# Expert results of a mixture-of-experts layer: rows scattered to token order, instead of tiles stored and gathered

## The chip, the core and the metric

One core of a Trainium2 chip runs one decoder layer for 512 tokens of 1024 values, in float32. The metric is the time of one execution on the device in microseconds (us), the median of several runs. The profile shows one execution on that core. Its engines are TensorE (PE in the rows, its weight loads PEld), VectorE (DVE), ScalarE (ACT), GpSimd (POOL) and SyncE (SP, its queue SPq), and 16 DMA engines that all queues share.

## What is computed

Only the last part of the layer matters here: a mixture of 32 experts in 4 groups of 8. Each token takes the best group and in it the two best experts, so there are 512 x 2 = 1024 (token, expert) rows.

```python
p_group, g_idx = lax.top_k(group_probs, 1)
...
top_vals, top_idx = lax.top_k(sel_logits, TOP_K_IN_GROUP)
weights = jax.nn.softmax(top_vals, axis=-1) * p_group
...
    h = jax.nn.silu(jnp.einsum('nd,edf->nef', t, w_g[sl])) * jnp.einsum('nd,edf->nef', t, w_u[sl])
    h = h * combine[:, sl, None]
    out = out + jnp.einsum('nef,efd->nd', h, w_d[sl])
...
x = layer_norm(DEEPNORM_ALPHA * x + gate2 * moe, ln2_g[l], ln2_b[l])
```

An expert's weights are 3 MB (gate and up 1024 x 256 each, down 256 x 1024).

## The kernel before

Attention and the first norm run until about 510 us, then the routing, then the experts. The routing sorts the 1024 rows by expert. Experts 0 to 5 have fixed places; the others are put in order of their number of rows, on the chip.

The experts are worked off in 12 units (line 124): eight pairs, whose tile of 128 rows is 64 of each of two experts, and four quads, with 32 of each of four. A unit has `ntl` tiles: three for most, two for the pair `pairs[7]` and for the quads 2 and 3. Tile 0 is always computed. Tiles 1 and 2 are computed under a condition (`tiles`, line 1278): only if the largest number of rows of an expert in the unit, read from `fl`, exceeds what the tiles before hold. ScalarE and VectorE work on all tiles in any case (`act_h`, `h_copy`, `y_evac`, lines 1228 to 1264); those of a tile not computed hold nothing that is read later. Rows beyond an expert's third tile go through a loop for overflow (line 1469), which runs only if there are any.

For each unit (loop at line 1381): `gate_up` (line 1224), `act_h`, transposes `h_tr` and their copies `h_copy` (1247), `down` (1254), and `y_evac` (1264), which multiplies by `gate2` and puts tile t into the buffer `yb[t]`. There is one such buffer for each t, shared by all units. Where a pair follows a pair, `gate_up` of the next unit is put ahead of the unit's transposes.

The weights go through 15 granules of 1 MB (`load_gran`, lines 862 and 865); each is loaded again when its matmuls are done. All these loads are issued by SP, with conditions for experts without rows.

TensorE, SP and GpSimd run this stage in the order in which the code is written (`manual_schedule(engines=MS)`, lines 1194 and 1332). The order of VectorE and ScalarE is chosen by a scheduler at compile time, except in the last unit. An engine whose next instruction waits runs nothing behind it. Semaphores are put in by the framework, from the accesses to each tile.

Results travel so:

- `Ys`, a tensor in DRAM, has a row for each place of each tile, and 640 rows for the overflow loop. `zero_fill` (133) writes zeros into all rows that may stay unwritten; SP issues it between the attention heads.
- `y_store0` (1270) and `y_store` (1276) store `yb[0]`, and `yb[1]` and `yb[2]` under a condition, on SP's queue, in between the weight loads. The last unit is not stored: it is added from `yb` through a selection matrix.
- `y_rows` (1097 to 1123), called in unit 1, computes for each token the two rows of `Ys` that it needs, `posy` and as integers `posyi`.
- At the end GpSimd gathers these rows into `gt`, 128 rows of 4 KB in each of eight indirect DMAs (1518), VectorE adds them with their weights (1538) for one half of the columns, TensorE for the other, and the second norm follows (`moments`, `normed`, `gain`, `shift`).

GpSimd has besides in this stage: `norm_rows` (line 1294, small loads) and `select_rows` (1308 to 1315, the selection matrix of the last unit), both called at the end of the loop's pass for unit 9, and `scaled` (1460) at the end. VectorE's copies `split_rows` (1300) need the loads of `norm_rows`; TensorE's transposes `select_tr` (1321) in the last unit need the selection matrix.

Of the kernel before, what the change touches and what calls it, by code (L numbers as in the profile page):

```python
# [11 lines left out]
F32 = mybir.dt.float32  # L12
F32R = mybir.dt.float32r
BF16 = mybir.dt.bfloat16
# [21 lines left out]
YO = 14 * 192 + 2 * 128 + 8 * 96 + 8 * 64  # L36
NY = YO + 640
QR = 384
# [14 lines left out]
def tile_layer(ctx: ExitStack, tc: tile.TileContext, x, c, positions, w_ada, b_ada, w_in, mla_q_norm_g, w_q_up,  # L53
# [18 lines left out]
    def tmp(tag, shape, dtype=F32, name=None):  # L72
        return mp.tile([P] + shape, dtype, name=name or tag, tag=tag, bufs=2)
# [51 lines left out]

    Ys = dr.tile([NY, D], F32, name="Ys")
    zero = [(u.row + P, (u.ntl - 1) * P) for u in (pairs + quads)[:-1]]
    zero += [(quads[-1].row, P * quads[-1].ntl)] + [(lo, P) for lo in range(YO, NY, P)]

    def zero_fill(n):  # L130
        for lo, m in zero[:n]:
            to = Ys[lo:lo + m, :].rearrange("r (h n) -> (r h) n", h=2).rearrange("(p a) n -> p a n", a=max(1, m // 64))
            SP.dma_start(to, zt[0:min(P, 2 * m)].unsqueeze(1).to_broadcast([min(P, 2 * m), max(1, m // 64), 512]))
        del zero[:n]
# [553 lines left out]

    zero_fill(6)
    branch(w_branch_sb, osh, osl, lambda a, m: DVE.tensor_tensor(part(gat, m), a, part(gat, m), ALU.mult), "ysb")  # L690
# [16 lines left out]

    oml = gran("Q1", [HP, S], F32R, "oml")
    attention(score_mla, vm, omh, oml, 54 / 32.0, 1, before=lambda h: (fq.until(f"qu{h}"), zero_fill(4)))
    fq.drain()  # L710

# [346 lines left out]
    posy = cp.tile([P, NT, 2], F32, name="posy")  # L1058
    posyi = cp.tile([P, NT, 2], I32, name="posyi")

# [34 lines left out]
    def y_rows():  # L1095
# [27 lines left out]
        DVE.tensor_copy(posyi, posy)  # L1123

# [45 lines left out]
    def overflow_list():  # L1170
        over = ovt
        for k in range(TOV):
            lim = float(OV0 + CAP * k)
            DVE.tensor_scalar(over[:, 0, :, k], cnt[:, 0, :], lim, None, ALU.is_gt)
            DVE.tensor_scalar(over[:, 2, :, k], cnt[:, 1, :], lim, None, ALU.add)
            DVE.memset(over[:, 2, 1, k:k + 1], float(NSLOT - CAP) - lim)
            DVE.tensor_scalar(over[:, 3, :, k], cnt[:, 0, :], lim, None, ALU.subtract)
            DVE.tensor_scalar(over[:, 4, :, k], yo[:, 1, :], lim, None, ALU.add)
# [86 lines left out]

    def y_rows_of(u, t):
        return Ys[u.row + P * t:u.row + P * t + P, :]
# [64 lines left out]
    with tc.manual_schedule(engines=MS):  # L1332
# [48 lines left out]
        for n, u in enumerate(units):  # L1381
# [88 lines left out]
    with tc.If(total > 0):  # L1470
        with tc.For_i(0, total) as it:
# [36 lines left out]
            POOL.indirect_dma_start(out=Ys[:, :], out_offset=bass.IndirectOffsetOnAxis(ap=oii[0:64], axis=0), in_=yo[0:64], in_offset=None,  # L1508
                                    bounds_check=NY - 1, oob_is_err=False)


    ALL = MS | {mybir.EngineType.DVE, mybir.EngineType.Activation}
    with tc.manual_schedule(engines=ALL):
        gts = []
        for t in range(NT):
            gt = gran(etags[10 + t], [2, D], F32, f"gt{t}")
            for j in range(2):
                POOL.indirect_dma_start(out=gt[:, j, :], out_offset=None, in_=Ys[:, :],
                                        in_offset=bass.IndirectOffsetOnAxis(ap=posyi[:, t, j:j + 1], axis=0),
                                        bounds_check=NY - 1, oob_is_err=False)  # L1520
            gts.append(gt)
# [134 lines left out]
```

## Time and profile before

| what | value |
|---|---|
| median of 3 runs | 825.21 us (820.85 to 825.68) |
| the profiled execution's own time | 827.33 us |
| its span on the core | 825.6 us |
| mean granted clock of TensorE | 0.929 of full speed |
| TensorE, VectorE, ScalarE, GpSimd busy | 84%, 64%, 30%, 26% of the span |
| DMA packets | 195.15 MB, mean 236 GB/s |

The shares are means over stages that differ. Times in the profile count from the span's start. A busy time of TensorE holds pipelined matmuls, so it is not its use at its peak. In rows of one instruction or of several merged ones the columns are start (us), duration (us), engine, line, operation, output and input, number, and in brackets the idle time just before it with what ended that.

### The profile page before, as it was taken

Reading aid. Unit: us, or ns where it says so; the run is one execution under the profiler, and the core shown is the slowest. Engines: PE = TensorE matmul, PEld = TensorE weight load, DVE = VectorE, ACT = ScalarE, POOL = GpSimd, SP = SyncE. Lnnn points to the kernel's source line nnn. Section 1 sums busy time; section 2 is a strip of 40 time slices with the busy share of each in tenths; the row PEclk is TensorE's granted clock in tenths of the full one; section 3 lists DMA queues with packets and bytes.
Section 4 is the critical chain, followed back from the end, with each engine's and each line's share of the span. In section 5 each row is a group of like instructions: output and inputs, shape, how many; then the busy total and the mean of one; then the engine's idle time right before and its main releaser. Section 6 shows DMA issues by size and latency. Waiting matters only on the chain. (4 is left out here: it accounts for less than half of the span.)

```text
span 825.6 us, 10607 instructions
## 1 busy us (share of the span) xinstructions
PE 691.5 (84%) x3201; PEld 426.7 (52%) x3201; DVE 524.3 (64%) x1083; ACT 249.7 (30%) x545; POOL 217.8 (26%) x269
## 2 busy tenths in 40 slices
PE   5789999999999798999989665777889779977880
PEld 3568877677776464666668553432333223322330
DVE  3995366867746857876596766664834715543297
ACT  2123244333435434443231324342201101111411
POOL 5546022322333312200363440300000000028174
PEclk9999999999999898999999867698999889999995
DMA  9964365547612793331549348788999998899942
GB/s 266 257 178 129 111 223 197 191 153 249 207 32 66 272 363 120 89 124 54 202 180 359 124 144 286 247 292 293 389 410 417 400 415 325 298 357 402 349 183 102
DMA packets 92109, 195.15 MB, mean 236 GB/s; under 512 B 11421, under 2 KB 53498, under 8 KB 86154
## 3 DMA queue, kind: packets, MB, share of 16 engines
q1 hardware_dynamic: 88544, 182.71, 62.5%
q0 software_dynamic: 3424, 11.57, 4.0%
q8 instruction: 36, 0.59, 0.3%
q14 instruction: 31, 0.25, 0.1%
q10 hardware_dynamic: 74, 0.03, 0.0%
HBM read 173.30 MB, written 35.67 MB: 253 GB/s over the span
## 5 line engine op out<-in xcount | busy, mean ns | idle before, releaser
L1224 PE MATMUL pgu<-ex,xT 128*64 128x512 f32 (+1 forms) x608 | 119.5, 615 | 17.7 <-DMA ex<-in_w_exp_up_dram 10.6
L1224 PEld LDWEIGHTS pgu<-ex,xT 128*64 128x64 f32 (+1 forms) x608 | 49.1, 129 | 82.3 <-issue 71.1
L330 PE MATMUL acc<-uh,whi 128*128 128x512 f32 x224 | 90.9, 406 | 0.0
L330 PE MATMUL acc<-uh,wlo 128*128 128x512 f32 x224 | 88.3, 394 | 0.4 <-DVE wlo L321 0.4
L330 PE MATMUL acc<-ul,whi 128*128 128x512 f32 x224 | 87.6, 391 | 0.0
L1254 PE MATMUL py<-ex,hT 128*64 128x512 f32 (+1 forms) x304 | 66.2, 668 | 17.7 <-DVE hT L1247 12.8
L577 POOL TENSOR_TENSOR w<-be,sc 128x128 f32<-128x128 f32 (+3 forms) x32 | 39.6, 1239 | 135.6 <-DVE sc L575 113.0
L1232 ACT ACTIVATE sl<-pgu 128x256 f32<-128x256 f32 x33 | 11.4, 383 | 173.7 <-PE pgu L1224 154.3
L1294 POOL DMA_DIRECT2D lraw<-in_ln_g_dram x4 | 2.0, 510 | 203.2 <-DVE lraw L1291 203.2
L330 PEld LDWEIGHTS acc<-uh,whi 128*128 128x128 f32 x224 | 42.1, 188 | 14.6 <-issue 4.4
L321 DVE TENSOR_TENSOR wlo<-raw,whi 128x1024 fp32r<-128x1024 f32 x27 | 34.4, 1272 | 21.8 <-ACT whi L320 21.6
L330 PEld LDWEIGHTS acc<-uh,wlo 128*128 128x128 f32 x224 | 42.0, 188 | 11.2 <-DVE wlo L321 2.0
L1254 PEld LDWEIGHTS py<-ex,hT 128*64 128x64 f32 (+1 forms) x304 | 16.9, 135 | 59.2 <-issue 29.2
L443 DVE SCALAR_TENSOR_TENSOR macc<-ra,rtx,macc 128x1024 f32<-128x1024 f32 x28 | 38.4, 1394 | 13.5 <-DMA ra<-in_w_ada_dram 13.4
L330 PEld LDWEIGHTS acc<-ul,whi 128*128 128x128 f32 x224 | 42.2, 188 | 7.9 <-issue 0.2
L1233 DVE TENSOR_TENSOR sl<-pgu,sl 128x256 f32<-128x256 f32 x33 | 12.9, 419 | 43.3 <-ACT sl L1232 43.3
L320 ACT CAST whi<-raw 128x1024 fp32r<-128x1024 f32 x27 | 28.4, 1051 | 29.5 <-PE acc L330 14.2
L1247 DVE COPY hT<-phT 128x256 f32<-128x256 f32 x33 | 13.2, 419 | 32.6 <-PE phT L1239 19.7
L575 DVE TENSOR_TENSOR_SCAN sc<-al 128x127 f32<-128x127 f32 (+3 forms) x32 | 27.1, 849 | 10.5 <-ACT al L571 8.6
L817 PE MATMUL oh<-wo,mixh 128*128 128x512 f32 x64 | 28.7, 497 | 5.8 <-DVE wo L801 5.8
L536 PE MATMUL px<-ident,w 128*128 128x128 f32 x160 | 28.9, 280 | 5.3 <-POOL w L577 2.1
L1217 DVE COPY xT<-XRA 128x128 f32 (+1 forms) x30 | 7.6, 252 | 34.7 <-PE pgu L1224 29.7
(491 smaller groups left out, 1515.5 us busy)
## 6 DMA issues: line engine op xcount, KB each, us to landing
ex<-in_w_exp_gate_dram SPq DMA_DIRECT2D x64, 512.0 KB
ex<-in_w_exp_up_dram SPq DMA_DIRECT2D x64, 512.0 KB
ex<-in_w_exp_down_dram SPq DMA_DIRECT2D x32, 1024.0 KB
ra<-in_w_ada_dram SPq DMA_DIRECT2D x16, 1024.0 KB
raw<-in_w_in_dram SPq DMA_DIRECT2D x12, 1024.0 KB
Ys<-dq SPq DMA_DIRECT2D x10, 1024.0 KB
ada<-in_w_ada_dram SPq DMA_DIRECT2D x16, 512.0 KB
rwo<-in_w_out_dram SPq DMA_DIRECT2D x6, 1024.0 KB
```

The costliest lines, as they stand in the source:

```text
L320: ACT.copy(hi, w)
L321: DVE.tensor_tensor(lo, w, hi.bitcast(F32), ALU.subtract)
L330: PE.matmul(a, w_[:, k, :], part(u_, k), start=(k == 0 and n == 0), stop=(k == nk - 1 and n == 2))
L443: DVE.scalar_tensor_tensor(o, v, cact[:, k, 0:1], o, ALU.mult, ALU.add)
L536: PE.transpose(px[:, kt * P:(kt + 1) * P], w[:, kt * P:(kt + 1) * P], ident)
L575: DVE.tensor_tensor_scan(sc[:, 0:W - 1][:, ::-1], al[:, 1:W][:, ::-1], al[:, 1:W][:, ::-1], 1.0, ALU.mult, ALU.bypass)
L577: POOL.tensor_tensor(w[:, 0:W], be[:, 0:W], sc[:, 0:W], ALU.mult)
L817: PE.matmul(a, u_, w_[:, k % 4, :], start=first and n == 0, stop=last and n == 2)
L1224: PE.matmul(ps_t[rows, :], xT[u, t][:, k, rows], ew[e, k // 4][:, :, k % 4, :], start=(k == 0), stop=(k == KD - 1))
L1233: DVE.tensor_tensor(sl, ps_t[:, DE:2 * DE], sl, ALU.mult)
L1247: DVE.tensor_copy(hT[u, min(t, 1)][:, t // 2], phT[:, o:o + 256].rearrange("p (k n) -> p k n", k=2))
L1254: PE.matmul(pys[nh][rows, :], hT[u, min(t, 1)][:, t // 2, k, rows], ew[e, 2][:, k, nh * 512:(nh + 1) * 512], start=(k == 0), stop=(k == 1))
```

## The change

- `Ys` becomes 1024 rows in token order: row j*512 + token holds the result of the token's j-th expert. The overflow loop has a tensor `Yv` of 640 rows of its own. Both are filled with zeros, in 13 fills.
- `y_rows`, `overflow_list` move from unit 1 to unit 0. A new `y_index` and `y_index_out` invert `posy` with eight small matmuls: `yix[p, c]` says which row of the new `Ys` is place p of tile c, and is out of bounds for places without a row.
- Instead of SP's stores, GpSimd scatters each tile of the first 11 units, all their `ntl` tiles without a condition, 31 in all: one indirect DMA for a tile, with the tile's column of `yix`; rows out of bounds are left out.
- Unit 0's scatters are put behind the call of `y_index_out`, at its end.
- At the end SP loads `gt` with eight plain loads of 128 rows; the gathers go.
- If the overflow loop has run, its rows are loaded and scattered too.

```diff
-    Ys = dr.tile([NY, D], F32, name="Ys")
-    zero = [(u.row + P, (u.ntl - 1) * P) for u in (pairs + quads)[:-1]]
-    zero += [(quads[-1].row, P * quads[-1].ntl)] + [(lo, P) for lo in range(YO, NY, P)]
+    Ys = dr.tile([2 * S, D], F32, name="Ys")
+    Yv = dr.tile([NOVR, D], F32, name="Yv")
+    zero = [(y, lo) for y, n in ((Ys, 2 * S), (Yv, NOVR)) for lo in range(0, n, P)]
...
+    def y_index():
+        p8 = posy.rearrange("p t j -> p (t j)")
+        POOL.iota(trow.rearrange("p (t j) -> p t j", j=2), [[P, NT], [S, 2]], base=0, channel_multiplier=0, allow_small_or_imprecise_dtypes=True)
+        DVE.tensor_scalar(yhl[:, 0, :], p8, 1.0 / P, -0.49609375, ALU.mult, ALU.add)
+        DVE.tensor_scalar(yhl[:, 0, :], yhl[:, 0, :], MAGIC, None, ALU.add)
+        DVE.tensor_scalar(yhl[:, 0, :], yhl[:, 0, :], MAGIC, None, ALU.subtract)
+        DVE.scalar_tensor_tensor(yhl[:, 1, :], yhl[:, 0, :], -float(P), p8, ALU.mult, ALU.add)
+        lo = tmp("al", [8, P], BF16, "lo2")
+        DVE.tensor_tensor(lo, iot.unsqueeze(1).to_broadcast([P, 8, P]), yhl[:, 1, :].unsqueeze(2).to_broadcast([P, 8, P]), ALU.is_equal)
+        hi = tmp("be", [8, 3, NYT], BF16, "hi2")
+        DVE.tensor_tensor(hi[:, :, 0, :], iot[:, 0:NYT].unsqueeze(1).to_broadcast([P, 8, NYT]), yhl[:, 0, :].unsqueeze(2).to_broadcast([P, 8, NYT]), ALU.is_equal)
+        DVE.tensor_scalar(hi[:, :, 1, :], hi[:, :, 0, :], pcol, None, ALU.mult)
+        DVE.tensor_tensor(hi[:, :, 2, :], hi[:, :, 0, :], trow.unsqueeze(2).to_broadcast([P, 8, NYT]), ALU.mult)
+        return lo, hi
+
+    def y_index_out(lo, hi):
+        px = pt("z", 2, "pyx")
+        for n in range(8):
+            PE.matmul(px[:, 0:3 * NYT], lo[:, n, :], hi[:, n], start=(n == 0), stop=(n == 7))
...
+        DVE.tensor_tensor(yix, px3[:, 2], yf[:, 1], ALU.add)
...
-    def y_store0(u):
-        SP.dma_start(y_rows_of(u, 0), yb[0])
-
-    def y_store(u):
-        if u.ntl > 1:
-            n = SP.value_load(fl[0:1, u.fl:u.fl + 1], min_val=0, max_val=S)
-            for t in range(1, u.ntl):
-                SP.dma_start(y_rows_of(u, t), yb[t], cond=(n > u.r * t), cond_hint=False)
+    def scatter(y, c):
+        POOL.indirect_dma_start(out=Ys[:, :], out_offset=bass.IndirectOffsetOnAxis(ap=yix[:, c:c + 1], axis=0), in_=y, in_offset=None,
+                                bounds_check=2 * S - 1, oob_is_err=False)
+
+    def y_store(u, ts):
+        for t in ts:
+            if t < u.ntl:
+                scatter(yb[t], u.row // P + t)
...
             y_evac(u, 0, py0)
-            if more:
-                y_store0(u)
+            if more and n:
+                y_store(u, (0,))
...
-            if n == 1:
+            if n == 0:
                 y_rows()
+                lohi = y_index()
                 overflow_list()
...
-            if more:
-                y_store(u)
+            if more and n:
+                y_store(u, (1, 2))
...
                 gate_up(un, 0, ps0, range(4, KD))
+                if n == 0:
+                    y_index_out(*lohi)
                 act_h(un, 0, ps0)
                 if n == 0:
                     more_tiles(1)
+                    y_store(u, (0, 1, 2))
...
             for j in range(2):
-                POOL.indirect_dma_start(out=gt[:, j, :], out_offset=None, in_=Ys[:, :],
-                                        in_offset=bass.IndirectOffsetOnAxis(ap=posyi[:, t, j:j + 1], axis=0),
-                                        bounds_check=NY - 1, oob_is_err=False)
+                SP.dma_start(gt[:, j, :], Ys[j * S + t * P:j * S + (t + 1) * P, :])
```

NYT, the number of 128-row pieces of the old `Ys`, is 38.

## Rows read from the trace of the kernel before

**Rows 1.** Busy us by stretch of the expert stage; then clock, DMA share, GB/s

```profile
core 0: us, PE busy (x) PEld busy (x) DVE busy (x) ACT busy (x) POOL busy (x), PEclk, DMA share, GB/s
...
560.00:620.00 60.00, 50.65 (x250) 20.10 (x248) 32.26 (x104) 9.80 (x37) 0.00 (x0) 0.93 0.96 364
620.00:680.00 60.00, 49.23 (x241) 16.79 (x238) 25.33 (x73) 7.93 (x30) 0.00 (x0) 0.89 1.02 411
```

**Rows 2.** Timeline of TensorE, where it waits in units 1 to 5

```profile
577.23 2.75 PE L1254 MATMUL py<-ex,hT 128*64 128x512 f32 x8 [2.35 <-DVE hT L1247]
...
600.55 3.65 PE L1224 MATMUL pgu<-ex,xT 128*64 128x512 f32 x16 [1.68 <-DMA ex<-in_w_exp_up_dram]
605.63 17.35 PE L1224 MATMUL pgu<-ex,xT 128*64 128x512 f32 x78 [1.42 <-DMA ex<-in_w_exp_up_dram]
...
665.17 1.04 PE L1224 MATMUL pgu<-ex,xT 128*64 128x512 f32 x2 [3.40 <-DMA ex<-in_w_exp_up_dram]
667.74 6.63 PE L1224 MATMUL pgu<-ex,xT 128*64 128x512 f32 x14 [1.52 <-DMA ex<-in_w_exp_up_dram]
```

**Rows 3.** What writes `Ys` (duration min/median/max in ns), and SP's timeline

```profile
L133 SPq DMA_DIRECT2D Ys<-dq x17: 546/814/2220, 272.9 to 310.4; - x17
L1270 SPq DMA_DIRECT2D Ys<-w x11: 353/354/391, 549.7 to 772.3; - x11
...
L1276 SPq DMA_DIRECT2D Ys<-sc x11: 96/96/360, 557.2 to 774.9; - x11
...
645.13 0.36 SPq L1276 DMA_DIRECT2D Ys<-sc  x1
646.33 0.36 SPq L1276 DMA_DIRECT2D Ys<-rtx  x1
```

**Rows 4.** Waits of TensorE from 200 to 420 us, the longest in total

```profile
PE px L536 <- POOL w L577: 2.1, 1, 2.1
```

**Rows 5.** Timelines of VectorE and TensorE: index steps, and unit 0's end

```profile
514.15 1.21 DVE L1045 TENSOR_TENSOR lo<-iot,hlf 128x1024 bf16<-128x1024 f32 x1
...
550.77 1.27 DVE L1264 TENSOR_TENSOR rtx<-pgu,gate 128x512 f32<-128x512 f32 x2
...
558.76 6.55 PE L1224 MATMUL pgu<-ex,xT 128*64 128x512 f32 x16 [3.89 <-DVE sl L1233]
...
572.96 0.28 DVE L1107 TENSOR_TENSOR y<-rk,cnt 128x128 f32<-128x128 f32 x1
...
581.74 0.47 DVE L1122 TENSOR_REDUCE posy<-y 128x4 f32<-128x128 f32 x2
```

**Rows 6.** Timeline of VectorE: evacuations of units 3, 7 and 8, and the end

```profile
602.57 1.28 DVE L1264 TENSOR_TENSOR rtx<-pgu,gate 128x512 f32<-128x512 f32 x2
...
716.99 1.28 DVE L1264 TENSOR_TENSOR w<-py,gate 128x512 f32<-128x512 f32 x2
...
732.54 1.29 DVE L1264 TENSOR_TENSOR sc<-py,gate 128x512 f32<-128x512 f32 x2 [1.69 <-DMA Ys<-sc]
...
791.33 4.99 DVE L1538 SCALAR_TENSOR_TENSOR ex<-gt,wt,ex 128x512 f32<-128x512 f32 x2
...
799.00 1.53 DVE L1538 SCALAR_TENSOR_TENSOR ex<-gt,wt,ex 128x512 f32<-128x512 f32 x2
```

**Rows 7.** GpSimd's DMAs, issue to landing: gathers `xg` (L1133), stores `xhd` (L943), loads `lraw` (L1294)

```profile
518.52 1.01 POOL L1133 DMA_INDIRECT xg<-xhd,gidx  x1 [0.30 <-issue]
...
DMA to landing us min/median/max: 4.7/5.0/5.1
...
DMA to landing us min/median/max: 2.9/4.8/7.5
...
DMA to landing us min/median/max: 6.0/6.2/6.6
```

**Rows 8.** Timeline of GpSimd: `norm_rows` begins, `select_rows` ends

```profile
737.46 0.56 POOL L1294 DMA_DIRECT2D lraw<-in_ln_g_dram  x1 [203.23 <-DVE lraw L1291]
...
760.63 0.46 POOL L1315 TENSOR_TENSOR gate<-gate,rk 128x128 f32<-128x128 f32 x1
```

More of the change, by code (lines that the diff above doesn't have):

```diff
@@ L36 @@
 YO = 14 * 192 + 2 * 128 + 8 * 96 + 8 * 64
-NY = YO + 640
+NOVR = 640
+NY = YO + NOVR
+NYT = NY // P
 QR = 384
@@ L124, in tile_layer @@
     units = [pairs[0], pairs[1], pairs[2], quads[0], pairs[3], quads[1], pairs[4], pairs[5], pairs[6], pairs[7], quads[2], quads[3]]
-    Ys = dr.tile([NY, D], F32, name="Ys")
-    zero = [(u.row + P, (u.ntl - 1) * P) for u in (pairs + quads)[:-1]]
-    zero += [(quads[-1].row, P * quads[-1].ntl)] + [(lo, P) for lo in range(YO, NY, P)]
+    Ys = dr.tile([2 * S, D], F32, name="Ys")
+    Yv = dr.tile([NOVR, D], F32, name="Yv")
+    zero = [(y, lo) for y, n in ((Ys, 2 * S), (Yv, NOVR)) for lo in range(0, n, P)]
     def zero_fill(n):
-        for lo, m in zero[:n]:
-            to = Ys[lo:lo + m, :].rearrange("r (h n) -> (r h) n", h=2).rearrange("(p a) n -> p a n", a=max(1, m // 64))
-            SP.dma_start(to, zt[0:min(P, 2 * m)].unsqueeze(1).to_broadcast([min(P, 2 * m), max(1, m // 64), 512]))
+        for y, lo in zero[:n]:
+            SP.dma_start(y[lo:lo + P, :].rearrange("r (h n) -> r h n", h=2), zt.unsqueeze(1).to_broadcast([P, 2, 512]))
         del zero[:n]
@@ L687, in branch @@
             fq.add(name, load(m // 2), split(m), mm_run(lambda a, m=m: evac(a, m), 4, oh, ol))
-    zero_fill(6)
+    zero_fill(2)
     branch(w_branch_sb, osh, osl, lambda a, m: DVE.tensor_tensor(part(gat, m), a, part(gat, m), ALU.mult), "ysb")
@@ L708, in tile_layer @@
     oml = gran("Q1", [HP, S], F32R, "oml")
-    attention(score_mla, vm, omh, oml, 54 / 32.0, 1, before=lambda h: (fq.until(f"qu{h}"), zero_fill(4)))
+    attention(score_mla, vm, omh, oml, 54 / 32.0, 1, before=lambda h: (fq.until(f"qu{h}"), zero_fill(2)))
     fq.drain()
@@ L1058, in tile_layer @@
     posy = cp.tile([P, NT, 2], F32, name="posy")
-    posyi = cp.tile([P, NT, 2], I32, name="posyi")
     row0 = identb.bitcast(F32)[:, 0:32]
@@ L1122, in y_rows @@
             DVE.reduce_sum(posy[:, :, j], pm_[:, j], axis=AX.X)
-        DVE.tensor_copy(posyi, posy)
+    yix = msk_mla.bitcast(I32)[:, 0:NYT]
+    yhl = msk_mla.bitcast(F32)[:, 40:56].rearrange("p (a n) -> p a n", a=2)
+    trow = msk_mla.bitcast(F32)[:, 56:64]
+    def y_index():
[16 more added lines that the diff above has]
+            PE.matmul(px[:, 0:3 * NYT], lo[:, n, :], hi[:, n], start=(n == 0), stop=(n == 7))
+        px3 = px[:, 0:3 * NYT].rearrange("p (a n) -> p a n", a=3)
+        yf = gate1[:, 800:800 + 2 * NYT].rearrange("p (a n) -> p a n", a=2)
+        DVE.tensor_scalar(yf[:, 0], px3[:, 0], -float(4 * NY), float(4 * NY), ALU.mult, ALU.add)
+        DVE.tensor_tensor(yf[:, 1], px3[:, 1], yf[:, 0], ALU.add)
+        DVE.tensor_tensor(yix, px3[:, 2], yf[:, 1], ALU.add)
     XAB = [gran(t, [4, NPAD], F32, f"X{t}") for t in ("RA", "RB")]
@@ L1177, in overflow_list @@
             DVE.tensor_scalar(over[:, 3, :, k], cnt[:, 0, :], lim, None, ALU.subtract)
-            DVE.tensor_scalar(over[:, 4, :, k], yo[:, 1, :], lim, None, ALU.add)
+            DVE.tensor_scalar(over[:, 4, :, k], yo[:, 1, :], lim - YO, None, ALU.add)
         has = over[:, 0].rearrange("p e k -> p (e k)")
@@ L1264, in y_evac @@
                 DVE.tensor_tensor(y[:, cols_], pys[nh], gate2[:, cols_], ALU.mult)
-    def y_rows_of(u, t):
-        return Ys[u.row + P * t:u.row + P * t + P, :]
-    def y_store0(u):
-        SP.dma_start(y_rows_of(u, 0), yb[0])
-    def y_store(u):
-        if u.ntl > 1:
-            n = SP.value_load(fl[0:1, u.fl:u.fl + 1], min_val=0, max_val=S)
-            for t in range(1, u.ntl):
-                SP.dma_start(y_rows_of(u, t), yb[t], cond=(n > u.r * t), cond_hint=False)
+    def scatter(y, c):
[5 more added lines that the diff above has]
+                scatter(yb[t], u.row // P + t)
     def tiles(u, f, run, t=1):
@@ L1507, in tile_layer @@
                 DVE.tensor_tensor(yo[0:64, nh * 512:(nh + 1) * 512], py[0:64], gate2[0:64, nh * 512:(nh + 1) * 512], ALU.mult)
-            POOL.indirect_dma_start(out=Ys[:, :], out_offset=bass.IndirectOffsetOnAxis(ap=oii[0:64], axis=0), in_=yo[0:64], in_offset=None,
-                                    bounds_check=NY - 1, oob_is_err=False)
+            POOL.indirect_dma_start(out=Yv[:, :], out_offset=bass.IndirectOffsetOnAxis(ap=oii[0:64], axis=0), in_=yo[0:64], in_offset=None,
+                                    bounds_check=NOVR - 1, oob_is_err=False)
+        for i in range(NOVR // P):
+            yo = tmp("wlo", [D], F32, "yv")
+            SP.dma_start(yo, Yv[i * P:(i + 1) * P, :])
+            scatter(yo, YO // P + i)
     ALL = MS | {mybir.EngineType.DVE, mybir.EngineType.Activation}
```

1 line of the change is left out of this document (removed).

## The prediction

> **What bounds the kernel now.** I read the busy table by stretch first, because the change lives in one stage: the experts, from about 520 us on. From 560 to 680 us the 16 DMA engines are busy all the time (shares 0.96 and 1.02, 411 GB/s), while TensorE is busy 50.65 and 49.23 of 60 us [rows 1]. So the expert weights set the pace, but TensorE is close behind it: a load removed gives back only what TensorE now waits for loads. The order of TensorE's work shows these waits: 1.68 and 1.42 us before the matmuls at 600.55 and 605.63, 3.40 and 1.52 before those at 665.17 and 667.74, together 8.0 us [rows 2]. The last stage, from 790 on, is a chain on VectorE that starts when it adds the first gathered rows, at 791.33 [rows 6].
>
> Times below are in the profiled execution's own frame, 827.33 us (span 825.6 and 1.7 around it). The median of the runs shown is 825.21, 2.1 lower, so 2.1 comes off at the end. A measurement of this kernel can tell about 1%, 8.3 us, from no change.
>
> **1. Bytes.** 15 tiles of 512 KB are stored now: 11 first tiles, and four conditional ones. Of the conditional stores most cost SP 0.096 us, which is a skip; one that transfers takes 0.36, as the first two of the four, at 645.13 and 646.33 [rows 3]. That is 7.86 MB in the load queue. The scatters write real rows only. The 512 tokens have 1024 rows in these 15 tiles and the last unit's one, 64 per tile on average, so half of the bytes go: 3.9 MB, 9.6 us at 411 GB/s [rows 1]. Seven of the stores are issued before TensorE's wait at 665, from 549.7 to 646.33, so by then half of 3.67 MB, 1.84 MB, less are ahead of it: 4.5 us off the 8.0 of waits. What is saved where TensorE doesn't wait I count as nothing. Bounds: 0 (if masked rows cost as much as real ones, see rivals) and 8.0.
>
> **2. Zero fill.** 17 fills of 14.2 MB become 13 of 6.8 MB, at 273 to 312 us [rows 3]. In that stage TensorE's longest wait in total is one of 2.1 us for GpSimd, and none is for a DMA [rows 4]: 0, bounds -2 and 0.
>
> **3. Rows and index table in unit 0.** `y_rows` (16 instructions of 0.17 to 0.49 us, first at 572.96 and last at 581.74, 4.3 us in sum) moves from unit 1 into unit 0 [rows 5]. `y_index` adds one compare of 128x1024, 1.21 us as at 514.15, three of 304 columns at a third of that, and four small ones of 0.2: 3.2 us. Then TensorE's eight small matmuls (taken as 0.1 each) and three small VectorE steps. VectorE ends unit 0's last evacuation at 550.77+1.27 = 552.0, so the table is there at 552.0+4.3+3.2+0.8+0.6 = 561, and the first scatter can go at 562. TensorE holds the eight matmuls in order, and behind them stands unit 2's first matmul, which waits for VectorE's `act_h` and starts at 558.76 now [rows 5]. It starts at about 562: +3 us, bounds 0 (VectorE finds earlier gaps) and +7.5 (none). Unit 1 is rid of `y_rows`, between whose steps the copy of hT was late by 2.35 us for TensorE at 577.23 [rows 2]: -2.35. Sum of the part: +0.65.
>
> **4. The scatters, each behind the one before.** This decides. 31 scatters go to GpSimd's queue, which runs in the written order. All write the one tensor `Ys`, at rows known only on the chip; I take it that each waits until the one before has landed. The trace of before has no two such writes, so this is a choice (0.85). The price of one, p, is its time to landing and the step to the next. Nearest rows: the eight gathers of the same form and 512 KB, 4.7 to 5.1 us, with 0.30 us between two; plain stores of 512 KB from GpSimd, 2.9 to 7.5, median 4.8; 4 KB loads from GpSimd beside the expert weights, 6.0 to 6.6 [rows 7]. So p lies between 2.9 and 7.5+0.3 = 7.8. I take the median gather, 5.0+0.3 = 5.3, for full and empty scatters alike: empty ones move less, but beside full queues.
>
> The Trainium skill, "DMA: Bandwidth & Descriptors" (Two DMAs through the same engine are not ordered), says that a queue gives two DMAs no order and that the issuing engine has to wait for the first one's completion; no row here shows two dependent DMAs. It goes with the wait that I assume. The same page (Anatomy of one DMA) fits a transfer from GpSimd at 2.0 us and its bytes by 436 GB/s, an estimate of 3.2 us for 512 KB; the gathers' 4.7 to 5.1 don't agree. By that p the rival of short scatters, below, would hold.
>
> Who waits for the queue: VectorE's evacuation into `yb[t]` has to wait for the scatter of that buffer one unit before, and behind it in VectorE's queue stand the copies that TensorE needs. In units 0 to 2, nine scatters start at 562 and end at 562+9p; unit 3's last evacuation (602.57) needs the ninth [rows 6]. It is late by 9p-40.6: 7.1 us at 5.3. That lag takes the place of TensorE's waits for loads, since loads go on meanwhile: of the 8.0 us only 0.9 stay to be gained. So parts 1 and 4 give -0.9 together (-4.5 at p up to 4.9; above 5.4 a loss).
>
> After that the queue drains, until units 7 to 9 come close together. Unit 7's first evacuation ends at 718.3 [rows 6]. From there seven scatters lie ahead of unit 9's second one, which is issued at 718.3+7p = 755.4. Unit 8's evacuations lose a wait of 1.69 us at 732.54 for a store [rows 6], and the queue is not behind there at 5.3 by more than 0.5: -1.7 (0 at a longer p).
>
> **5. What GpSimd holds behind them.** `norm_rows` and `select_rows` come after unit 9's scatters in the written order. Now they start at 737.46, in unit 8, and take 23.6 us, to 761.1 [rows 8]. Behind a scatter issued at 755.4 (1.0 us on GpSimd) they end at 780.0. Only then go unit 10's two scatters, although its tiles are ready long before. The last lands at 718.3+7p+24.6+2p = 790.6. The loads of `gt` on SP wait for it; the first takes between 2.9 and 7.5 us (the plain stores of rows 7), the low end being nearer, since the weights are in by then. With 4 VectorE has its first rows at 794.6, against 791.33: +3.3, that is 9p-44.4. Now the gathers take GpSimd's time there, and VectorE's first add of gathered rows runs beside GpSimd's last `scaled`; that this goes is between 0 and -3.5 (4.99 us for two adds that take 1.53 at 799.00) [rows 6], and I take 0, as VectorE waits longer.
>
> **Sum.** +0.65 -0.9 -1.7 +3.3 = +1.4. SP also loses its waits for evacuations; loads behind them are held by buffers of the same tiles, so 0, bounds -2 and 0. 827.3+1.4-2.1 = 826.6 us: no change that can be measured.
>
> **Rivals.**
> *The queue falls behind (slower).* One mechanism: scatters in full DMA queues take what the 4 KB loads took, p = 6.2+0.3 = 6.5 [rows 7]. Unit 3 is late by 17.9, less the 8.0 of waits: +9.9; the end by 9x6.5-44.4 = +14.1; the store's wait stays. With +0.65 that is +24.7: 850 us. It decides from p = 5.6, where the sum reaches 1%: 0.65+1.8+6.0 = 8.4. For it: DMA shares of 1.0 where most scatters go. Against: more than half of them carry no row, and a VectorE that waits leaves the queues emptier. Chance 0.29.
>
> *The queue is never behind (faster).* Either scatters don't wait for each other, or the 16 empty ones land in the least store's 2.9+0.3. Then the nine scatters, six of them empty, take 3x5.3+6x3.2 = 35.1, less than 40.6. The seven from 718.3 take 4x5.3+3x3.2 = 30.8, GpSimd's own work 24.6 and the last two 8.5: 782.2, with a load of 4 still before VectorE asks. Sum: +0.65-4.5-1.7, and up to -3.5 at the end: -5.6 to -9, 816 to 820. For it: the least store, and 16 scatters that carry nothing. Against: the 4 KB loads needed 6.0. Chance 0.26.
>
> *Masked rows are moved all the same (the bytes don't fall).* 31 x 0.524 = 16.3 MB instead of 7.86 would cost 8.4 MB at 411 GB/s, +20 us: 847. The trace has no masked row. Chance 0.05.
>
> **How the numbers follow.** Forecast 0.40 (own range 818 to 834), queue behind 0.29, queue never behind 0.26, masked rows 0.05. Faster by over 1% (under 817): most of half of the third case, and some of the unpriced end, 0.21. Slower by over 1% (over 833.5): 0.29+0.05. Same: 0.45. The range leaves out under 0.1 below 812, where the fast case has reached all its bounds, and over 0.1 above 851, just past the slow case's centre.
>
> **What would show it.** Right: a scatter's time to landing near 5.0; GpSimd's queue waiting for the scatter before; VectorE waiting for `Ys` stores in units 1 to 3; `norm_rows` and `select_rows` at 756 to 780 instead of 737 to 761; the first `gt` load landing near 795; 3.9 MB less written in the stage. Wrong: scatters a microsecond apart (then the fast case), landings over 5.6 us (the slow one), or TensorE's waits for loads at 600 and 665 unchanged while VectorE waits for nothing.

## The result, and the profile after

The changed kernel takes 866.28 us (865.93 to 867.83, 4 runs) against 823.12 us (820.85 to 825.68, 4 runs) beside it: a ratio of 1.0527, 95% interval 1.0484 to 1.057. It is slower by 43 us, and outside of the predicted range. The profiled execution took 865.96 us, with a span of 864.2.

The place to look first is GpSimd's order of work, since the scatters went there. Its timeline in the kernel after (start, duration, operation; in brackets the idle time before it and what ended that):

```profile
559.95 1.02 POOL L1297 DMA_INDIRECT Ys<-w,msk_mla  x1 [31.48 <-ACT xT L1247]
569.70 0.99 POOL L1297 DMA_INDIRECT Ys<-sc,msk_mla  x1 [8.73 <-DMA Ys<-w,msk_mla]
572.46 0.97 POOL L1297 DMA_INDIRECT Ys<-rtx,msk_mla  x1 [1.77 <-DMA Ys<-sc,msk_mla]
581.91 0.97 POOL L1297 DMA_INDIRECT Ys<-w,msk_mla  x1 [8.48 <-DMA Ys<-rtx,msk_mla]
590.56 0.97 POOL L1297 DMA_INDIRECT Ys<-sc,msk_mla  x1 [7.68 <-DVE w L1294]
600.43 0.97 POOL L1297 DMA_INDIRECT Ys<-rtx,msk_mla  x1 [8.90 <-issue]
609.18 0.98 POOL L1297 DMA_INDIRECT Ys<-w,msk_mla  x1 [7.78 <-issue]
...
632.29 0.97 POOL L1297 DMA_INDIRECT Ys<-w,msk_mla  x1 [7.90 <-DMA Ys<-rtx,msk_mla]
636.59 0.97 POOL L1297 DMA_INDIRECT Ys<-sc,msk_mla  x1 [3.33 <-DVE xT L1247]
639.43 0.97 POOL L1297 DMA_INDIRECT Ys<-rtx,msk_mla  x1 [1.86 <-DMA Ys<-sc,msk_mla]
...
791.66 0.97 POOL L1297 DMA_INDIRECT Ys<-sc,msk_mla  x1 [8.07 <-DMA Ys<-w,msk_mla]
792.62 0.58 POOL L1321 DMA_DIRECT2D lraw<-in_ln_g_dram  x1
...
815.83 0.45 POOL L1342 TENSOR_TENSOR gate<-gate,rk 128x128 f32<-128x128 f32 x1
816.62 1.11 POOL L1297 DMA_INDIRECT Ys<-w,msk_mla  x1 [0.34 <-issue]
```

One scatter costs GpSimd 1 us of its own, and then the next stands still until it has landed: "8.73 <-DMA Ys<-w" ahead of the second. (The releaser named is the last one by the profile. Among these nine gaps, those that name a VectorE step or "issue" are as long as the others, and within a unit such gaps are gone in the run without the chain, below.) The nine scatters of units 0 to 2 start at 559.95 and the tenth at 632.29: (632.29-559.95)/9 = 8.04 us for each, from 2.76 to 9.87. The time from a scatter's issue to its landing, for all 31:

```profile
DMA to landing us min/median/max: 2.1/6.9/10.3
```

`norm_rows` begins at 792.62 and `select_rows` ends at 816.3, where the kernel before had 737.46 and 761.1 [rows 8].

What this does to the other engines shows in the table of waits from 520 to 864 us (total, times, longest):

```profile
PE phT L1269 <- DVE sl L1263: 43.0, 4, 25.4
...
POOL Ys L1297 <- DMA Ys<-rtx,msk_mla: 36.7, 5, 8.5
POOL Ys L1297 <- DMA Ys<-w,msk_mla: 35.6, 5, 8.8
...
POOL Ys L1297 <- DMA Ys<-sc,msk_mla: 27.6, 6, 6.7
DVE rtx L1294 <- DMA Ys<-rtx,msk_mla: 27.4, 5, 7.6
...
PE py L1284 <- DVE hT L1277: 23.4, 6, 10.2
...
DVE lrow L1327 <- DMA lraw<-in_ln_b_dram: 21.7, 1, 21.7
DVE sc L1294 <- DMA Ys<-sc,msk_mla: 20.0, 4, 8.0
...
DVE w L1294 <- DMA Ys<-w,msk_mla: 6.2, 2, 3.7
...
PE pgu L1254 <- DMA ex<-in_w_exp_up_dram: 4.0, 3, 2.4
```

In the kernel before, from 520 to 826 us, TensorE's rows of that table were these:

```profile
PE py L1254 <- DVE hT L1247: 12.8, 6, 3.9
...
PE pgu L1224 <- DMA ex<-in_w_exp_up_dram: 10.6, 6, 3.4
...
PE phT L1239 <- DVE sl L1233: 3.1, 3, 1.2
```

GpSimd now waits 99.9 us for scatters to land (36.7 + 35.6 + 27.6), VectorE 53.6 (27.4 + 20.0 + 6.2) for the buffers that they read, where it waited 8.4 for stores before. TensorE's waits for `up` loads fall from 10.6 to 4.0 us. In their place its waits for VectorE rise from 3.1 to 43.0 us (`sl`) and from 12.8 to 23.4 (hT). The two timelines show the same, first VectorE's evacuations and its later steps:

```profile
581.25 1.29 DVE L1294 TENSOR_TENSOR rtx<-pgu,gate 128x512 f32<-128x512 f32 x2 [7.08 <-DMA Ys<-rtx,msk_mla]
...
599.79 1.29 DVE L1294 TENSOR_TENSOR sc<-py,gate 128x512 f32<-128x512 f32 x2 [8.04 <-DMA Ys<-sc,msk_mla]
...
798.18 0.73 DVE L1327 CAST lrow<-lraw 36x1024 fp32r<-36x1024 f32 x1 [21.74 <-DMA lraw<-in_ln_b_dram]
...
833.76 1.53 DVE L1571 SCALAR_TENSOR_TENSOR ex<-gt,wt,ex 128x512 f32<-128x512 f32 x2
```

and TensorE's order at the same places:

```profile
582.93 3.44 PE L1284 MATMUL py<-ex,hT 128*64 128x512 f32 x8 [10.15 <-DVE hT L1277]
...
611.92 0.70 PE L1269 MATMUL phT<-ident,sl 128*128 128x128 f32 x2 [15.68 <-DVE sl L1263]
...
799.30 0.70 PE L1269 MATMUL phT<-ident,sl 128*128 128x128 f32 x2 [25.37 <-DVE sl L1263]
```

VectorE stands 7.08 us before the evacuation at 581.25, whose buffer is still being read, and the copy of hT that TensorE needs stands behind it: the wait of 2.35 us at 577.23 [rows 2] has become one of 10.15 at 582.93. In the same way the product `sl` stands behind the wait of 8.04 us at 599.79 and a further one of 5.73, and TensorE waits 15.68 us until 611.92. At 798.18 VectorE has waited 21.74 us for the norm rows. The first add of gathered rows moves from 791.33 [rows 6] to 833.76. Last, the table by stretch, which answers [rows 1] (after the stretch: its length, busy us of PE, PEld, DVE, ACT, POOL; clock, DMA share, GB/s):

```profile
560.00:620.00 60.00, 31.00 (x164) 12.25 (x162) 23.04 (x67) 7.81 (x30) 7.79 (x8) 0.75 0.93 341
...
740.00:780.00 40.00, 22.12 (x120) 10.15 (x116) 15.36 (x41) 4.77 (x18) 4.87 (x5) 0.84 1.01 397
780.00:800.00 20.00, 0.70 (x2) 0.32 (x2) 1.79 (x4) 0.00 (x0) 9.05 (x15) 0.50 0.50 182
```

TensorE does 31.00 us of work from 560 to 620, where it did 50.65, and next to none from 780 to 800. Its granted clock in the first stretch is 0.75 of full speed instead of 0.93, which comes on top of the waits. In slices of 5 us the clock is 1.00 from 590 to 595, and 0.50, the lower of its two levels (1.2 and 2.4 GHz), from 600 to 615; TensorE did nothing between 596.2 and 611.9.

### The profile page after: what moved, and what is told of

It is laid out like the page before. It is cut to its first block, busy times and chain, and to the rows that moved or that the text cites. A ratio compares the mean times of both kernels' runs of the same rounds, so it can differ in the third digit from the quotient of the medians.

```text
span 864.2 us, 10586 instructions
## 1 busy us (share of the span) xinstructions
PE 687.5 (80%) x3209; PEld 428.6 (50%) x3209; DVE 520.3 (60%) x1093; ACT 249.7 (29%) x545; POOL 240.9 (28%) x293
## 3 DMA queue, kind: packets, MB, share of 16 engines
HBM read 173.30 MB, written 28.33 MB: 233 GB/s over the span
## 5 line engine op out<-in xcount | busy, mean ns | idle before, releaser
L1254 PE MATMUL pgu<-ex,xT 128*64 128x512 f32 (+1 forms) x608 | 117.7, 622 | 13.7 <-DVE rtx L1294 6.1
L1284 PE MATMUL py<-ex,hT 128*64 128x512 f32 (+1 forms) x304 | 63.1, 666 | 28.1 <-DVE hT L1277 23.4
L1269 PE MATMUL phT<-ident,sl 128*128 128x128 f32 x32 | 8.1, 341 | 45.5 <-DVE sl L1263 43.0
L1297 POOL DMA_INDIRECT Ys<-w,msk_mla x11 | 10.9, 990 | 113.6 <-DVE w L1294 37.3
L1294 DVE TENSOR_TENSOR sc<-py,gate 128x512 f32<-128x512 f32 x24 | 16.0, 686 | 30.3 <-DMA Ys<-sc,msk_mla 20.0
L1269 PEld LDWEIGHTS phT<-ident,sl 128*128 128x128 f32 x32 | 5.0, 207 | 57.4 <-DVE sl L1263 46.6
```

The source lines that it names most:

```text
L1254: PE.matmul(ps_t[rows, :], xT[u, t][:, k, rows], ew[e, k // 4][:, :, k % 4, :], start=(k == 0), stop=(k == KD - 1))
L1269: PE.transpose(phT[:, o + k * P:o + (k + 1) * P], h[:, k, :], ident)
L1284: PE.matmul(pys[nh][rows, :], hT[u, min(t, 1)][:, t // 2, k, rows], ew[e, 2][:, k, nh * 512:(nh + 1) * 512], start=(k == 0), stop=(k == 1))
L1294: DVE.tensor_tensor(y[:, cols_], pys[nh], gate2[:, cols_], ALU.mult)
```

## Experiments

In all of them the pairs of times were taken on one chip beside the kernel before, whose medians there were 822.6 to 824.2 us. The runs were made in four groups on four chips, so between groups the ratios compare better than the times.

### Taking the chain away, and moving the norm rows

The first run gives each scatter its own view of `Ys`, so that the framework orders it only against the loads of the end. The rows of two scatters are never the same ones.

```diff
+    Yd = dram_disjoint_views(Ys[:, :], NYT)
...
-        POOL.indirect_dma_start(out=Ys[:, :], ...
+        POOL.indirect_dma_start(out=Yd[c], ...
```

> The changed kernel, but each scatter writes through its own view of the token-ordered array, which the dependency tracker takes as disjoint from the others; only the loads of the end wait for all of them. Theory A (each scatter waits for the landing of the one before, 7 to 10 us a step beside full load queues, and so GpSimd falls behind and VectorE with it): scatters of one unit leave within 1 to 3 us of each other, VectorE's waits for scatter buffers (27.4 + 20.0 + 6.2 us in the changed kernel) fall below 10 us together, the wait of 21.7 us ahead of the copy of the norm rows goes too since GpSimd is on time, and the time is 814 to 826 us. Theory B (the indirect traffic or its queue costs the time, in whatever order): 850 us or more.

Measured: 822.58 us, ratio 0.9991 (0.9968 to 1.0015). The whole loss is gone, by 866.28-822.58 = 43.7 us. GpSimd's timeline of this run:

```profile
559.48 1.03 POOL L1298 DMA_INDIRECT Ys<-w,msk_mla  x1 [31.48 <-ACT xT L1248]
560.82 0.99 POOL L1298 DMA_INDIRECT Ys<-sc,msk_mla  x1 [0.31 <-issue]
562.12 0.97 POOL L1298 DMA_INDIRECT Ys<-rtx,msk_mla  x1 [0.30 <-issue]
...
736.85 0.97 POOL L1298 DMA_INDIRECT Ys<-w,msk_mla  x1 [7.11 <-DVE w L1295]
738.13 0.97 POOL L1298 DMA_INDIRECT Ys<-sc,msk_mla  x1 [0.30 <-issue]
...
746.40 0.49 POOL L1322 DMA_DIRECT2D lraw<-in_ln_g_dram  x1 [4.29 <-DMA Ys<-w,msk_mla]
...
748.78 0.48 POOL L1322 DMA_DIRECT2D lraw<-in_ln_b_dram  x1 [1.90 <-DMA Ys<-sc,msk_mla]
```

The scatters of a unit now leave 1.3 us apart, and VectorE's waits for their buffers sum to 9.7 us. A scatter takes as long to land as before, even a little longer (7.6 us at the median against 6.9). So not the scatter's own slowness costs the time, but that each was paid for one after the other. One expectation failed: the wait ahead of the norm rows did not go, it is 17.2 us instead of 21.7. VectorE in this run, and in the run below that has no chain and also the loads earlier:

```profile
754.36 0.82 DVE L1328 CAST lrow<-lraw 36x1024 fp32r<-36x1024 f32 x1 [17.18 <-DMA lraw<-in_ln_b_dram]
```

```profile
742.64 0.69 DVE L1328 CAST lrow<-lraw 36x1024 fp32r<-36x1024 f32 x1 [6.90 <-PEq L1308]
```

Two more runs put the loads of the norm rows ahead of unit 9's scatters, with the chain and without it.

```diff
                 xcopy(n + 1, 2)
+            if n == 3 + NOV // 2:
+                norm_rows()
...
-                norm_rows()
                 select_rows()
```

> The changed kernel, but the loads of the norm rows stand on GpSimd ahead of unit 9's scatters instead of behind them; the chain of scatters stays. Theory A with the block at the norm rows as a cost of its own: the loads leave near 777 us instead of 793, the wait ahead of the copy falls from 21.7 to some 10 us, and the time to 853 to 859 us. Rival (the 21.7 us only stand beside GpSimd's late end, which sets the time anyway): 863 to 868 us.

> Both edits together, no chain and the norm rows ahead of unit 9's scatters. Theory A: with no chain GpSimd is on time, so the order of the norm rows is worth 0 to 3 us beside the run without a chain alone: 813 to 825 us. If the block at the norm rows is a cost of its own, independent of the chain: 10 us or more under the run without a chain alone. Theory B: 840 us or more.

Measured: 860.47 us with the chain (ratio 1.0462, 1.0418 to 1.0507), and 816.09 without (0.9927, 0.9906 to 0.9949). The place of these eight small loads is worth 5.8 and 6.5 us, beside the chain or without it. So it is a cost of its own, if a small one; both expectations of the time were off, the first by 1.5 us, the second by 3.5. (The loads left at 775.9 and the wait ahead of the copy fell to 10.0 us, as expected.) The 21.7 us of the wait are not its price: most of them ran beside what was late anyway. A control makes the same move in the kernel before, where GpSimd has no stores.

> The kernel before, with the loads of the norm rows moved to the same place as in the experiments on the changed one; a control. Theory A (the place matters only behind late scatters; in the kernel before the copy of the norm rows waited for no load): 821 to 826 us, the same as before. Rival (the place is a gain by itself, and the 6.5 us that it gave without the chain have nothing to do with scatters): 815 to 818 us.

Measured: 823.54 us, ratio 0.9985 (0.9956 to 1.0014). Nothing changes: there the copy did not wait for a load.

### The queue without the chain

To part the chain from the queue, the kernel before had its plain stores issued by GpSimd in `y_store0` and in `y_store`, with the register of the condition. These go to disjoint rows, and none waits for another by its data.

```diff
-        SP.dma_start(y_rows_of(u, 0), yb[0])
+        POOL.dma_start(y_rows_of(u, 0), yb[0])
...
-            n = SP.value_load(fl[0:1, u.fl:u.fl + 1], min_val=0, max_val=S)
+            n = POOL.value_load(fl[0:1, u.fl:u.fl + 1], min_val=0, max_val=S)
...
-                SP.dma_start(y_rows_of(u, t), yb[t], ...
+                POOL.dma_start(y_rows_of(u, t), yb[t], ...
```

> The kernel before, with its plain stores of the unit tiles issued by GpSimd instead of the load queue, nothing else changed: disjoint rows, no wait between stores, gathers at the end as before. Theory A (only the wait between stores costs): 817 to 827 us, GpSimd's stores land without holding each other. Theory B (stores from GpSimd's queue land late whatever they wait for, and hold the buffers): 840 us or more.

Measured: 822.82 us, ratio 0.9983 (0.9951 to 1.0014). The 15 stores that transfer cost nothing by going through GpSimd's queue; the other 16 are skipped here, as in the kernel before.

### Which scatters make the chain

Of the 31 scatters 16 belong to tiles that are not computed; every index in them is out of bounds. This run keeps the chain, and branches around those.

```diff
         for t in ts:
-            if t < u.ntl:
-                scatter(yb[t], u.row // P + t)
+            if t == 0:
+                scatter(yb[0], u.row // P)
+            elif t < u.ntl:
+                if u not in fpool:
+                    fpool[u] = POOL.value_load(fl[0:1, u.fl:u.fl + 1], min_val=0, max_val=S)
+                with tc.If(fpool[u] > u.r * t):
+                    scatter(yb[t], u.row // P + t)
```

> The changed kernel with its chain, but GpSimd branches around the scatters of the second and third tile of a unit where the unit has no such tile (the condition under which the kernel before stored them); what is left is a chain of some 16 to 20 scatters instead of 31. Theory A (every scatter, empty or not, costs one landing of 7 to 10 us in the chain): 11 to 15 steps fewer, GpSimd has 1 or 2 steps a unit of about 22 us and keeps up, VectorE's waits for scatter buffers fall from 53.6 to under 15 us, and the time to 818 to 832 us. Rival (an out-of-bounds scatter moves nothing and costs little; the full ones make the chain): 855 us or more.

Measured: 821.13 us, ratio 0.9956 (0.9939 to 0.9973). With 15 scatters the chain costs nothing that shows: 866.28-821.13 = 45.2 us were the price of 16 more links in it, transfers that carry nothing. VectorE's waits for scatter buffers are 13.9 us, under the 15 expected. GpSimd in this run:

```profile
559.60 1.03 POOL L1297 DMA_INDIRECT Ys<-w,msk_mla  x1 [31.46 <-ACT xT L1247]
572.16 0.99 POOL L1297 DMA_INDIRECT Ys<-w,msk_mla  x1 [11.54 <-DVE w L1294]
...
636.86 0.97 POOL L1297 DMA_INDIRECT Ys<-sc,msk_mla  x1 [8.25 <-DMA Ys<-w,msk_mla]
645.69 0.97 POOL L1297 DMA_INDIRECT Ys<-rtx,msk_mla  x1 [7.86 <-DVE mp__6172 L1221]
```

In units 0 to 3 only the first tile is left, so GpSimd waits for VectorE's evacuation (11.54 us), no longer for a landing. In unit 4, with three real tiles, a step still takes 8.8 us (636.86 to 645.69). In the timeline after, the three full scatters of units 0 to 2 take 8.5 to 9.8 us, mean 9.0, and the six empty ones 2.8 to 9.9, mean 7.6. So an empty scatter in the chain costs nearly what a full one does. That the empty ones carry nothing is in the table of queues, GpSimd's queue in the kernel after, then in this run (packets, MB, share):

```profile
q0 software_dynamic: 6736, 11.57, 3.8%
```

```profile
q0 software_dynamic: 4432, 11.56, 3.9%
```

2304 packets go with the 16 scatters, 144 for each, and 0.01 MB.

### What sets the price of a step

If a step is the wait of a scatter among the loads, half the loads should make it cheaper. These two runs leave out half of the columns of the conditional expert loads, so the experts' weights from the third unit on are half old data; one has the chain, the other separate views.

```diff
-                SP.dma_start(t[:, s_], wsel(w_, KD)[:, 4 * q:4 * q + 4, :], **kw)
+                m = 2 if kw else 4
+                SP.dma_start(t[:, s_, 0:m], wsel(w_, KD)[:, 4 * q:4 * q + m, :], **kw)
...
-            SP.dma_start(t, wsel(w_exp_down, 2), **kw)
+            m = 1 if kw else 2
+            SP.dma_start(t[:, 0:m], wsel(w_exp_down, 2)[:, 0:m], **kw)
```

> The changed kernel with its chain, but the expert loads issued with a condition bring half of their columns (256 instead of 512 KB, 512 instead of 1024 KB), so half of the experts' weights from the third unit on are left out. Theory A' (the price of a step is the wait of the scatter behind outstanding loads): steps fall from 7 to 10 us to 3 to 5 us, VectorE's waits for scatter buffers from 53.6 to under 20 us, and the time is within 15 us of the run with half loads and no chain. Rival (a fixed price of a software transfer, whatever the load queues do): steps stay at 7 us or more, and the chain costs 30 us or more here too.

> The same half loads (half of the experts' weights from the third unit on left out) in the kernel without a chain: the base for the run beside it. 795 to 820 us by either theory; what counts is the difference, under 15 us by theory A', 30 us or more by the rival.

Measured: 826.9 us with the chain, 804.95 without. The difference is 22 us, half of the 43.7 at full loads; I had set 15 and 30 as the marks of the two theories, and it fell between. VectorE's waits for scatter buffers are 38.8 us, where theory A' had under 20. The landings lean to that theory all the same: from issue to landing it is now

```profile
DMA to landing us min/median/max: 2.1/4.2/9.4
```

against 6.9 at the median, and the nine scatters of units 0 to 2 take 52.1/9 = 5.8 us each (561.10 to 613.15) instead of 8.04, at a DMA share of 0.70 instead of 0.93 (560 to 620).

The kernel after shows the same within one trace. The step from 569.70 took 2.76 us at a DMA share of 0.61 (568 to 573), and the one from 636.59 took 2.84 at 0.03 (637 to 642), both for empty scatters. The loads of `norm_rows`, 4 KB each, needed 6.2 us at the median in the kernel before [rows 7], at a share of 1.03 (737 to 747). In the kernel after they leave from 792.6 on, at a share of 0.05 (790 to 795):

```profile
DMA to landing us min/median/max: 1.7/1.8/1.9
```

So the load on the DMA engines makes most of the price. Of the loss by the chain, half is left with half the loads; the loads of the norm rows also leave later in the run with the chain (752.6 instead of 730.4), so that rest is not the price alone.

### What is left to gain, and from where

Four runs put earlier edits together or do one part alone. The first has the branch and the move of `norm_rows`, the second the views on top of both.

> The changed kernel with its chain, the empty scatters branched around, and the norm rows ahead of unit 9's scatters. Theory A (the late norm rows cost some 6 us in every kernel whose GpSimd carries the stores): 6 us under the run that only branches around, 813 to 818 us. Rival (what is left of the chain sets the time): 819 to 823 us.

> The same with a view of its own for each scatter, so that no scatter waits for another. Theory A: with one to three scatters a unit the chain is hidden, so this is within 2 us of the run beside it, 812 to 818 us. Rival (the chain of full scatters still holds buffers): 4 us or more below it.

Branching around the empty scatters with the norm rows ahead of unit 9's: 813.51 us, ratio 0.9882 (0.9834 to 0.993), 1.2% faster than the kernel before. Separate views on top give 814.8 (0.9899, 0.9851 to 0.9947): no further gain, so a chain of 15 is hidden.

The third is the kernel before with its stores on GpSimd and the move of `norm_rows`.

> The kernel before with its plain stores issued by GpSimd, and the norm rows ahead of unit 9's stores; gathers, zero fills and bytes as before. Theory C (what the kernel without a chain gains over the kernel before comes from taking the stores out of the load queue's order, not from the scattering, the smaller fills or the plain loads of the end): 814 to 819 us. Rival (the gain is the scattering's own: fewer bytes and no gathers): 821 to 825 us.

Measured: 818.84 us, ratio 0.9946 (0.9914 to 0.9978), with plain stores, gathers and bytes as before. Against the control (823.54 us, ratio 0.9985, 0.9956 to 1.0014) that is 4.7 us by the medians and 3.2 by the ratios, for taking the stores out of the load queue's order alone. The two intervals overlap, so this is not clear of the noise. The other 5 us to 813.51 are the scattering's, the fills' or the plain loads'.

The fourth does part 3 alone, in the kernel before, with the new functions of the change copied in and their table unused.

```diff
-            if n == 1:
+            if n == 0:
                 y_rows()
+                lohi = y_index()
                 overflow_list()
...
                 gate_up(un, 0, ps0, range(4, KD))
+                if n == 0:
+                    y_index_out(*lohi)
```

> The kernel before with the rank reduction, the index table's VectorE and TensorE steps and the overflow list in unit 0 instead of unit 1, the table unused: part three of the prediction alone. The prediction's step: 0.7 us more, 822 to 826 us. Rival (VectorE's 15 us in unit 0 delay the units behind it, or the earlier place in unit 0 gains what unit 1 no longer has to do): outside of 820 to 827 us.

Measured: 829.35 us, ratio 1.0048 (1.0014 to 1.0082): part 3 costs about 4 us by itself (0.0048 x 823; 1.2 to 6.7 by the interval). The time lies in the rival's range, not in that of the prediction's step. TensorE in this run:

```profile
563.23 6.00 PE L1254 MATMUL pgu<-ex,xT 128*64 128x512 f32 x16 [1.63 <-DVE sl L1263]
...
580.67 2.82 PE L1284 MATMUL py<-ex,hT 128*64 128x512 f32 x8 [1.85 <-DVE hT L1277]
```

Unit 2's first matmul starts 4.5 us later than at 558.76 [rows 5], and the wait for hT goes only from 2.35 [rows 2] to 1.85.

In the traces every kernel with the smaller fills starts the output projection at 415.2 to 417.2 us, and every kernel with the fills of before at 420.1 to 422.1, which looked like a gain in the attention stage that I had put at 0. One run puts 14 fills of 512 KB back into the kernel of 813.51 us, into a tensor that nothing reads; another leaves the five fills of the overflow rows out (`((Ys, 2 * S),)` alone in that line). The first of them:

```diff
-    zero = [(y, lo) for y, n in ((Ys, 2 * S), (Yv, NOVR)) for lo in range(0, n, P)]
+    Yz = dr.tile([14 * P, D], F32, name="Yz")
+    zero = [(y, lo) for y, n in ((Ys, 2 * S), (Yv, NOVR), (Yz, 14 * P)) for lo in range(0, n, P)]
...
-    zero_fill(2)
+    zero_fill(11)
...
-    ... zero_fill(2)))
+    ... zero_fill(5)))
```

> The kernel with the empty scatters branched around and the norm rows early (813.5 us), with 14 more zero fills of 512 KB into a tensor that nothing reads, so that 14.2 MB are filled in the attention stage as in the kernel before instead of 6.8 MB. Theory D (the prediction's zero for the fills was wrong: the larger fills hold that stage's loads on the same queue): 817 to 821 us, and the first output-projection matmul 4 to 5 us later, near 421 us. The prediction's step (fills cost nothing there): 812 to 816 us.

> The same kernel (813.5 us) without the five fills of the overflow rows, which this input does not read; 4.2 MB filled. Theory D with a threshold (the fills cost only where they and the loads overfill the queues, and with 6.8 MB the DMA share there is 0.52 to 0.58): 812 to 815 us. Rival (each MB filled costs 0.7 us, as 5 us for 7.3 MB would have it): 810 to 812 us.

Measured: 814.99 us with the fills (ratio 0.99, 0.9874 to 0.9927) and 813.65 without the five (0.9898, 0.9851 to 0.9946). The first is inconclusive: its profiled execution does reach the output projection later (419.1 against 415.3), but the median rises by 1.5 us, inside the runs' scatter (812.71 to 817.74). That lies outside of theory D's range and inside that of the prediction's step; the intervals of the ratios would still leave room for 4 us.

Where the 5 us between 818.84 and 813.51 lie can be read from the two traces. From the first gather of `xg` to the end the run with plain stores takes 817.8-517.4 = 300.4 us, the run with scatters 811.9-510.8 = 301.1, and the run with the fills put back 815.8-515.1 = 300.7. So behind that point the scattering comes out even, with its fewer bytes, its index table and the plain loads of the end taken together; the 5 us lie ahead of it, where the fills are. These are single executions, and the medians show only 1.5 us for the fills, so the cause of the rest stays open.

## Why the prediction was wrong

The step that failed is the price p in part 4: I took 5.3 us for a scatter in the chain, and it was 8.04 in units 0 to 2. The mechanism was the prediction's own: the scatters do wait for each other (given 0.85), and the rival of a queue that falls behind is what happened, at a chance of 0.29. That rival too had p too low (6.5, 850 us); its terms at 8.04 would give 9 x 8.04 - 40.6 - 8.0 = 23.8 at unit 3 and 9 x 8.04 - 44.4 = 28.0 at the end, with 0.65 in all +52, against 38.6 between the two profiled executions. So with the price right the sum would have been slower by a wide margin. It overshoots for the most part by two things that it had at 0. The expert stage begins 5.9 us earlier (its first gather at 511.2 instead of 517.1), and from VectorE's first add of gathered rows to the end it is 3.8 us shorter. The two terms themselves come out near: unit 7's first evacuation ends 17.6 us later, so 23.5 counted from the stage's start, and from there to the first add it is another 24.8. The second agrees partly by luck, since the path at the end was another (part 5).

Why p came out low can be seen in the rows it was taken from. The gathers of [rows 7] run from 517 to 533 us, where the DMA engines are busy for 0.75 of the time (511 to 533); the scatters run at 0.93 to 1.01. Two rows were nearer in this respect. One I left out: at the end of the same trace eight gathers of 512 KB, of the same form, read `Ys` into `gt` at a DMA share of 1.00 (779 to 792).

```profile
L1518 POOL DMA_INDIRECT gt<-Ys,posyi x8: 986/1000/2315, 779.6 to 790.2; - x8
...
DMA to landing us min/median/max: 6.1/7.0/7.4
```

They stood beside each other, so part of that load was their own; but 7.0+0.3 as the price gives 17.1 at unit 3, 21.3 at the end and +39 in all. The other row were the small loads beside the expert weights, 6.0 to 6.6 [rows 7], which moved 4 KB. I had weighed them for less because empty scatters move less; but a transfer of 4 KB that needs 6 us says that the bytes don't set the price. The bound of 7.8 was nearer than the value taken, and the range (to 851) was cut below what that bound gives: 9 x 7.8 - 48.6 = 21.6, 9 x 7.8 - 44.4 = 25.8 and 0.65 are 48 us.

The prediction says that no row showed two dependent DMAs. One did, though not two writes: in the kernel before, GpSimd stood 18.50 us until 779.59 for a store of `Ys` before its first gather from it.

The Trainium skill's fit in "DMA: Bandwidth & Descriptors" (Anatomy of one DMA), which by the prediction's estimate gives 3.2 us, is further off still: 6.9 us at the median here. The Trainium skill says on the same page (Queues, rings and completion order) that a DMA engine takes turns between its queues by the packet. That alone doesn't make an empty scatter quick, since it still has its packets; the one at 572.46 kept the next waiting for 9.45 us. Whether the turns go by the packet no run here shows.

The other steps:

- **Part 1, bytes.** Right that rows out of bounds move nothing (the rival of masked rows falls). The 4.5 us less of TensorE's waits were not seen: its waits for `up` loads from 540 us on are 10.6 us in the kernel before, 8.3 in the kernel of 813.51 us, and 8.2 with plain stores, the bytes as before.
- **Part 2, zero fill.** In the time of the whole kernel 0 is within what could be measured (1.5 us, not clear of the noise). In the traces it is not: with the smaller fills the DMA share from 273 to 313 us falls from 1.00 to 0.55 and the output projection starts some 5 us earlier, although no long wait of TensorE named a DMA [rows 4]. The start of the expert stage scatters more, from 512.4 to 517.4 us with the fills of before and from 507.3 to 512.3 with the smaller ones.
- **Part 3, the index table.** +0.65 was mis-sized: about 4 us alone. The gain of 2.35 at hT hardly came (0.5), and the matmul was 4.5 us late instead of 3. The first scatter's start (562 predicted, 559.95 measured) came out right by luck: it went 13.9 us after the end of unit 0's last evacuation instead of 10, in a stage that began 5.9 us earlier.
- **Part 4, the end of unit 8's wait** (-1.7): lost in the chain.
- **Part 5.** Right in kind: `norm_rows` and `select_rows` came behind unit 9's scatters, at 792.6 to 816.3 instead of 756 to 780. Missed: the copy of the norm rows on VectorE waits for those loads and holds TensorE's work behind it. Three pairs of runs give 5.8, 6.5 and 7.6 us (821.13 to 813.51) for their place, and 5.4, 5.3 and 6.1 by the ratios. Wrong in the path at the end: VectorE's first add waited for no load of `gt`. Its last wait, 3.02 us before 831.36, was for TensorE, which had stood until 799.30 behind the norm rows. What the sum had between 0 and -3.5 and took as 0, the two adds of 4.99 us, was 1.53 at 833.76: the whole 3.5.
- **The stores leaving SP's queue**, put at 0 with bounds of -2 and 0, gave 3 to 5 us at the most, which is not clear of the noise.

## What to carry to other kernels

Before dependent transfers are put in a row, count them, empty ones too, and price each by the landing of a transfer in equally full queues, a small one too, not by its bytes and not by a quieter stretch. Then either tell the framework that they are disjoint or branch around those that carry nothing; here either took back all of 43 us. And when a queue may fall behind, look at everything that stands behind it in written order, down to small loads for which another engine waits.

## What the runs showed beyond that

- A scatter with all indices out of bounds still has 144 packets, and beside full load queues the next one waits nearly as long for it (7.6 us on the mean of six) as for a full one (9.0 on the mean of three).
- Loads from GpSimd that depend on no scatter waited for one: in the run without a chain the seventh and eighth load of the norm rows stood 4.29 and 1.90 us until the two scatters issued ahead had landed. In each case eight of GpSimd's transfers were under way, and the ninth waited for the first. The half-load run with the chain shows it again (one scatter and seven loads, then 2.49 us). But it is not the number under way that counts. In the run that branches around the empty scatters, the seventh load waited 4.59 us with one scatter and six loads ahead. With the norm rows moved as well, the sixth waited with one scatter and five loads:

```profile
733.97 0.49 POOL L1328 DMA_DIRECT2D lraw<-in_ln_b_dram  x1 [1.57 <-DMA Ys<-w,msk_mla]
```

Counted in written order, with the one or two scatters branched around between them, the load is the ninth from that scatter in both. That points to the framework's order and not to a limit of the chip; no run tries it by itself.

- The profile page's line of bytes written counts by the program and not by what moved: 28.33 MB after and 19.94 without the empty scatters, a difference of 16 tiles of 512 KB, while the queue moved 0.01 MB less. For bytes the table of queues is the one to read.
